# Cross attention's output projection by pairs of k-tiles and 1024 columns, six of its sixteen pieces by seven block products

## The chip, the cores and the metric

One NeuronCore of a Trainium2 chip runs the whole program. The metric is the device time of one launch in microseconds (us). Before the change it is 1568.43 us, the median of three runs (1567.85 to 1570.91).

## What is computed

One layer of an encoder on 256 tokens of width 2048, in float32: a token mixer, cross attention into 256 memory tokens, and a gated convolutional feed-forward network (FFN), each followed by a LayerNorm of `alpha * x + f(x)`. What matters here is the second of the three:

```python
def cross_attention(x, mem, wq, wk, wv, wo):
    ...
    s = jnp.einsum('bqhd,bkhd->bhqk', q, k).astype(jnp.float32) * (XATTN_HEAD_DIM ** -0.5)
    p = jax.nn.softmax(s, axis=-1)
    o = jnp.einsum('bhqk,bkhd->bqhd', p.astype(v.dtype), v).reshape(B, S, D_MODEL)
    return o @ wo

x = layer_norm(DEEPNORM_ALPHA * x + cross_attention(...), ln2_g, ln2_b)
x = layer_norm(DEEPNORM_ALPHA * x + conv_ffn(x, w_up, conv_w, conv_b, w_down), ln3_g, ln3_b)
```

The product `o @ wo` is 256 x 2048 times 2048 x 2048. It is called the output projection, or `xo`, below.

## The kernel before

**Products in three parts.** Every float32 factor of a large product is split into a high part of reduced precision (`hi`, a copy on ACT) and the rest (`lo`, a subtraction on DVE), `split`, lines 84 to 86. A product is then hi x hi + hi x lo + lo x hi, three matmuls of 512 columns each (`three`, line 358; the same three stand in `tok_steps`, lines 286 to 288).

**Slots.** The program is a list of slots (`slot`, line 141; `run`, line 184). A slot has one or more weight loads and a body of matmuls. A load (`Load`, line 96) is one transfer of at most 1 MB by SP's queue into one of three `raw` buffers, then its splits on ACT and DVE into buffers of a pool of 38 (`unit`, line 62). Ahead of each slot, `advance` (line 173) puts the transfers and splits of later loads into the program: `ahead` says how many loads beyond the slot's own are split by then. A background list (`pump`, line 165) puts a piece of attention work ahead of a slot. The framework's scheduler starts from this order and may move an instruction forward where, by its own reckoning, the engine would stand idle; each engine then runs its instructions in the order it was given.

**xo before.** `block_output` (line 924) makes four passes over 512 columns each; a pass has four pieces of 512 rows x 512 columns, one piece to a slot, with 24 matmuls (`tok_steps`, line 280: two blocks of 128 tokens, four k-tiles, three matmuls). `ahead` is 1. The last three pieces of the last pass share a slot, in which token block 0 is finished first (`last_ones`, line 308): its residual sum, its norm (`after_block`, line 1184) and its transposes (`inside`, line 1197, put in front of the last 12 matmuls) go on beside the matmuls of block 1. The heads of attention (`attend`, line 1063) are background work: the last two of four come ahead of the first and third slots of xo. Per pass and token block, `add_residual` (line 896) adds the accumulator to `res` and takes statistics.

**The FFN's down product.** `columns_1024` (line 372) goes by 1024 columns: a piece is two k-tiles x 1024 columns, that is, a 2 x 2 block matrix of weights against a 2 x 2 block matrix of activations (two token blocks by two k-tiles). An *eight* piece has 8 block products, 24 matmuls, one load of 1 MB. A *seven* piece uses Winograd's form of Strassen's method with 7 block products, 21 matmuls. It needs four sums of weight blocks and four sums of activation blocks. The weight sums come from a table in HBM that the program itself makes (`weight_sums`, line 332): six transfers on POOL's queue for each piece, of 0.25 or 0.5 MB, four of them with an add. So a seven piece has two loads, 0.75 MB of weights and 1 MB of sums. In a pass, four accumulators take the seven pieces' first four products; after the last seven piece, `early` (line 1241) adds these into `res` by one ACT and eight DVE operations. Four more accumulators hold the rest of the sums up to the pass's end, where `evac` (line 1262) adds them.

**Pacing of the table.** `make_sums` (line 350) issues one step of the table in each slot from `SUMS_FROM` = 18 on: a DVE copy that reads the slot's first weights, a POOL copy that reads its result, and then the transfer. There are 22 seven pieces, so 132 steps. In slot numbers, xo has slots 117 to 130, the FFN's up product 131 to 172, the first half's down product 173 to 192.

Of the kernel before, what the change touches and what calls it, by code (L numbers as in the profile page):

```python
# [11 lines left out]
F32R = mybir.dt.float32r  # L12
# [8 lines left out]
P = 128  # L21
D = 2048
S = 256
# [18 lines left out]
PAIRS = NF // 2 // HALVES  # L42
SEVEN = ((5, 5), (6, 6))

SUMS_FROM = 18


AFFINE_ON_DVE = ((0, 1, 0), (0, 1, 1), (1, 0, 1))
# [4 lines left out]
def tile_encoder_layer(ctx: ExitStack, tc: tile.TileContext, aps, out):  # L53
# [315 lines left out]
        cols = slice(i * 512, i * 512 + 512)  # L369
        return pair[0][:, cols], pair[1][:, cols]  # L370

    def columns_1024(pieces, sums, act, act_sums, seven, evac_early, evac, stagger):


        rest = [i for i in range(len(pieces)) if i not in seven]
        order, free = [], len(rest) - stagger
        for n, i in enumerate(seven):
            order += [i] + rest[n * free // len(seven):(n + 1) * free // len(seven)]
        order += rest[free:]
        one, two = {}, {}  # L380

        def into(d, key, tag):
            start = key not in d
            if start:
                d[key] = bank("acc", tag)
            return d[key], start

        def seven_body(i):
            def body(ws, ts):
                w11, (w22, w21) = ws[0], (block_of(ws[1], 0), block_of(ws[1], 1))  # L390
                (t1, t3), (t2, t4) = ([block_of(t, j) for j in range(2)] for t in ts)
                x, s = act[i], [(act_sums[i][:, 0, j], act_sums[i][:, 1, j]) for j in range(4)]
                stop = i == seven[-1]
                for key, a, b in ((1, x_of(x, 0, 0), w11), (5, s[0], t1), (6, s[1], t2), (7, s[2], t3)):
                    acc, start = into(one, key, "m")
                    three(acc, a, b, start, stop)
                for key, a, b in ((2, x_of(x, 0, 1), w21), (3, s[3], w22), (4, x_of(x, 1, 1), t4)):
                    acc, start = into(two, key, "g")
                    three(acc, a, b, start, False)
            return body  # L400

        def eight(ws, i, t, h, stop):
            acc, start = into(two, ((2, 3), (4, 8))[t][h], "g")
            for kk in range(2):
                three(acc, x_of(act[i], t, kk), block_of(ws[kk], 1 - h), start and kk == 0, stop and kk == 1)

        def eight_body(i):
            def body(ws):
                for t in range(2):
                    for h in range(2):  # L410
                        eight(ws, i, t, h, False)
            return body

        def last_body(*wss):
            ends = order[-stagger:]
            for t in range(2):
                for h in range(2):
                    for i, ws in zip(ends, wss):
                        eight(ws, i, t, h, i == ends[-1])
                    evac(t, h, two[((2, 3), (4, 8))[t][h]])  # L420

        for i in order[:-stagger]:
            if i in seven:
                slot([Load(pieces[i][:, 512:2048], cols=1536), LaterLoad(sums[i])], seven_body(i),
                     (lambda: evac_early(one)) if i == seven[-1] else None)
            else:
                slot([pieces[i]], eight_body(i))
        slot([pieces[i] for i in order[-stagger:]], last_body)


    ident = cp.tile([P, P], F32, name="ident")
# [575 lines left out]
                yield  # L1007


    memT, x1T, oT, x2T = [], [], [], []  # L1010
    KT, QT, V, PT = {}, {}, {}, {}

    def feature_into(d, h, j):
# [21 lines left out]
    def scores(h):  # L1035
# [24 lines left out]
        split(PT[h][:, 0], PT[h][:, 1], r3(tr, 2))  # L1060
        yield

    def attend(h):
        yield
        for i in range(2):
            o = bank("xo", "m")
            for jj in range(2):
                e = slice((2 * i + jj) * P, (2 * i + jj + 1) * P)
                for m in range(2):
                    for n, (x, y) in enumerate(PARTS):  # L1070
                        nc.tensor.matmul(o[:, jj * S:(jj + 1) * S], lhsT=V[h][x][:, m, e], rhs=PT[h][:, y, m],  # L1071
                                         start=m == 0 and n == 0, stop=m == 1 and n == 2)
            t = unit([P, 2, 2, S], F32R, name="act")
            split(t[:, :, 0], t[:, :, 1], r3(o, 2))
            oT.append(t)
        yield

# [49 lines left out]
        return lambda acc: conv(NF + f, acc, done)  # L1127

    def gate_sums(p):
        x = gated[p]  # L1130
        s = x[:, 2:4].rearrange("p a (b c) -> p (a b) c", b=2)
        x11, x21, x12, x22 = (x[:, k, t * P:t * P + P] for k in range(2) for t in range(2))
        for o, a, b, op in ((0, x21, x22, ALU.subtract), (2, x11, x21, ALU.subtract),
                            (1, s[:, 0], x11, ALU.subtract), (3, x12, s[:, 1], ALU.add)):
            nc.vector.tensor_tensor(s[:, o], a, b, op=op)
        gS[p] = unit([P, 2, 4, P], F32R, name="sums")
        split(gS[p][:, 0], gS[p][:, 1], s)

# [58 lines left out]
    def inside(left):  # L1197

        if left == 1:
            transpose(0, 0, 1, 2, 3)  # L1200
            advance_chunks(0, 0, 1, 0, 1, 2, 2, 3, 3)

    def norm_steps(t, c, i):

        if (t, c, i) == (0, 3, 1):
            standardise(n2, 0, 1)
            transpose(1, 0)
            advance_chunks(1, 0, 0)
            standardise(n2, 1, 1)
        elif (t, c, i) == (1, 0, 0):  # L1210
            standardise(n2, 2, 1)
            transpose(1, 1)
            advance_chunks(1, 1, 1)
            standardise(n2, 3, 1)
        elif (t, i) == (1, 0) and c < 3:
# [12 lines left out]

    def down_piece(key):
        half, g, p = key  # L1230
        return aps["down"][(2 * half + g) * PAIRS + p]

    def down(half):
# [1 line left out]
        if half:  # L1235
            n3["gb"], n3["params"] = [], [None, None]
        for g in range(2):
            def z_of(t, h, g=g):
                return res[:, t, (2 * g + h) * 512:(2 * g + h + 1) * 512]

            def early(b, z=z_of):

                def add(t, h, x, op=ALU.add):
                    y = z(t, h)
                    nc.vector.scalar_tensor_tensor(y, in0=y, scalar=1.0 if half else ALPHA, in1=x,
                                                   op0=ALU.mult, op1=op)

                def add_more(t, h, x, op):
                    nc.vector.tensor_tensor(z(t, h), z(t, h), x, op=op)

                u = unit([P, 2, 512], name="usum")
                nc.scalar.copy(u[:, 0], b[1])
                add(0, 0, b[1])
                add(0, 1, b[5])
                add(1, 1, b[5])
                nc.vector.tensor_tensor(u[:, 0], u[:, 0], b[6], op=ALU.add)
                nc.vector.tensor_tensor(u[:, 1], u[:, 0], b[7], op=ALU.add)
                add_more(0, 1, u[:, 0], ALU.subtract)
                add(1, 0, u[:, 1])
                add_more(1, 1, u[:, 1], ALU.subtract)  # L1260

            def evac(t, h, acc, g=g, z=z_of):
# [8 lines left out]
            columns_1024([down_piece((half, g, p)) for p in range(PAIRS)],  # L1271
                         [lambda key=(half, g, p): made[key] for p in range(PAIRS)],
                         Part(gT, half * PAIRS), Part(gS, half * PAIRS), list(range(SEVEN[half][g])), early, evac,
                         4 if half and g else 2)
            if half and g == 0:
                then(lambda: load_gb(n3, 2))

    for half in range(HALVES):
# [20 lines left out]
    return w.reshape(k // 512, 4, P, c // 512, 512).transpose(3, 0, 2, 1, 4).reshape(-1, P, 2048)  # L1299


def _by_block(w):


    w = w.reshape(HALVES, PAIRS, 2, P, 2, 2, 512).transpose(0, 4, 1, 3, 2, 5, 6)
    return w[:, :, :, :, (0, 0, 1, 1), (1, 0, 1, 0)].reshape(-1, P, 2048)


# [8 lines left out]
def _layout(i):  # L1317
# [19 lines left out]
    a["xo"] = _by_column(i["xo_w"][0])  # L1337
    a["up"] = _by_feature(i["ffn_up"][0])
    a["down"] = _by_block(i["ffn_down"][0])
# [23 lines left out]
```

## Time and profile before

| | |
|---|---|
| median of three runs | 1568.43 us |
| the profiled execution's own time | 1569.4 us |
| its span in the profile | 1567.6 us |
| PE (TensorE matmul) busy | 1547.9 us, 99% |
| PEld (its weight loads) busy | 1334.5 us, 85% |
| DVE (VectorE) busy | 1110.2 us, 71% |
| ACT (ScalarE) busy | 807.4 us, 52% |
| POOL (GpSimd) busy | 170.8 us, 11% |
| DMA | 362.78 MB, mean 231 GB/s |

PE is TensorE's matmuls, whose ends are modelled: a matmul of 512 columns stands in the trace with 389 ns, and the next one starts before that is over. So what a matmul costs in a full stream is read from the distance of the starts.

### The profile page before, as it was taken

What the parts mean: (1) busy time and instruction counts of PE and PEld (TensorE: products, weight loads), DVE (VectorE), ACT (ScalarE), POOL (GpSimd) and SP (SyncE); (2) the same over time, 40 slices, a digit from 0 to 9 for tenths busy, and PEclk for the clock granted to TensorE, in tenths of its full rate; (3) what the DMA queues carried; (4) which work ended last, traced back from release to release, by engine and by line L of the source; (5) the groups of instructions that cost most, each with busy time, mean ns of one, the idle gap of its engine ahead of it and who ended that gap; (6) DMA issues with size and microseconds to landing.
All of it is one profiled execution on the core that took longest, in us unless ns stands there. A gap on an engine that the chain in (4) does not pass through costs nothing.

```text
span 1567.6 us, 21463 instructions
## 1 busy us (share of the span) xinstructions
PE 1547.9 (99%) x8258; PEld 1334.5 (85%) x8258; DVE 1110.2 (71%) x1715; ACT 807.4 (52%) x1187; POOL 170.8 (11%) x288
## 2 busy tenths in 40 slices
PE   9999999999999999999999999999999999999996
PEld 7888888888888888988889888888888888888875
DVE  6568468667765776555657888877778787777768
ACT  5453353456553344444436566666465555556542
POOL 0003113121211111111201220000000000000000
PEclk9999999999999999999999999999999999999998
DMA  8569668887879678767972986555686454545883
GB/s 310 189 239 282 206 230 263 225 256 252 240 193 310 242 232 256 216 192 228 311 253 82 256 271 225 220 194 213 245 321 249 189 192 184 188 177 203 284 322 116
DMA packets 65159, 362.78 MB, mean 231 GB/s; under 512 B 7832, under 2 KB 8224, under 8 KB 30624
## 3 DMA queue, kind: packets, MB, share of 16 engines
q1 hardware_dynamic: 48544, 314.21, 54.5%
q0 software_dynamic: 16512, 47.20, 15.1%
q8 instruction: 65, 1.06, 0.3%
q14 instruction: 38, 0.31, 0.1%
HBM read 359.27 MB, written 48.24 MB: 260 GB/s over the span
## 4 chain that ended last, share of the span: by engine, by line
PE 95%; DVE 2%; DMA 2%; ACT 0%; issue 0%; SPq 0%; DVEq 0%; ACTq 0%
PE acc L224 35%; PE acc L226 18%; PE acc L286 8%; PE acc L287 8%; PE acc L288 8%; PE acc L361 4%; PE acc L362 4%; PE acc L360 4%; DMA raw<-wsum 1%; PE xs L1041 1%; PE xo L1071 1%; PE lev L664 1%; DMA raw<-in_down_dram 0%; PE acc L235 0%; DVE wlo L86 0%; PE acc L242 0%
## 5 line engine op out<-in xcount | busy, mean ns | idle before, releaser
L86 DVE TENSOR_TENSOR wlo<-raw,whi 128x1024 fp32r<-128x1024 f32 (+1 forms) x562 | 666.9, 1213 | 190.4 <-ACT whi L85 166.7
L85 ACT CAST whi<-raw 128x1024 fp32r<-128x1024 f32 (+1 forms) x562 | 566.1, 1043 | 222.6 <-PE acc L287 38.6
L224 PE MATMUL acc<-act,whi 128*128 128x512 f32 x2384 | 573.3, 392 | 2.0 <-DVE act L86 1.8
L224 PEld LDWEIGHTS acc<-act,whi 128*128 128x128 f32 x2384 | 438.8, 189 | 88.6 <-DVE act L86 2.3
L226 PEld LDWEIGHTS acc<-act,wlo 128*128 128x128 f32 x2384 | 306.9, 191 | 12.2
L226 PE MATMUL acc<-act,wlo 128*128 128x256 f32 x2384 | 310.6, 283 | 0.0
L286 PE MATMUL acc<-whi,act 128*128 128x512 f32 x448 | 175.7, 392 | 0.0
L288 PE MATMUL acc<-whi,act 128*128 128x512 f32 x448 | 174.5, 389 | 0.0
L287 PE MATMUL acc<-wlo,act 128*128 128x512 f32 x448 | 174.4, 389 | 0.0
L355 POOL COPY marks<-marks 128x1 f32<-128x1 f32 x132 | 76.1, 580 | 628.8 <-DVE marks L354 628.8
L246 ACT COPY half<-acc 128x256 f32<-128x256 f32 x144 | 52.9, 368 | 114.3 <-PE acc L226 113.4
L288 PEld LDWEIGHTS acc<-whi,act 128*128 128x128 f32 x448 | 84.1, 188 | 17.7
L286 PEld LDWEIGHTS acc<-whi,act 128*128 128x128 f32 x448 | 84.2, 188 | 16.9
L287 PEld LDWEIGHTS acc<-wlo,act 128*128 128x128 f32 x448 | 84.2, 188 | 16.7
L360 PE MATMUL acc<-whi,act 128*128 128x512 f32 x220 | 84.8, 390 | 1.2 <-ACT whi L85 1.2
L362 PE MATMUL acc<-whi,act 128*128 128x512 f32 x220 | 85.6, 389 | 0.0
L361 PE MATMUL acc<-wlo,act 128*128 128x512 f32 x220 | 85.4, 390 | 0.0
L1097 ACT ACTIVATE cy<-hbuf,convp 128x256 f32<-128x256 f32 x88 | 52.9, 601 | 44.2 <-DVE hbuf L247 44.2
L1098 DVE SCALAR_TENSOR_TENSOR cy<-hbuf,convp,cy 128x256 f32<-128x256 f32 x88 | 42.3, 482 | 25.5 <-ACT cy L1097 25.5
L286 PE MATMUL acc<-whi,mixT 128*128 128x512 f32 x128 | 50.0, 390 | 0.0
L360 PEld LDWEIGHTS acc<-whi,act 128*128 128x128 f32 x220 | 41.2, 188 | 10.2 <-ACT whi L85 1.6
L288 PE MATMUL acc<-whi,mixT 128*128 128x512 f32 x128 | 49.8, 389 | 0.0
(246 smaller groups left out, 1363.6 us busy)
## 6 DMA issues: line engine op xcount, KB each, us to landing
raw<-in_up_dram SPq DMA_DIRECT2D x88, 1024.0 KB, 4.8
raw<-in_w_ws_dram SPq DMA_DIRECT2D x29, 1024.0 KB, 6.4
raw<-in_w_xs_dram SPq DMA_DIRECT2D x24, 1024.0 KB, 6.7
wsum<-in_down_dram POOLq DMA_DIRECT2D x44, 512.0 KB, 9.8
raw<-wsum SPq DMA_DIRECT2D x22, 1024.0 KB, 5.4
raw<-in_down_dram SPq DMA_DIRECT2D x22, 1024.0 KB, 5.3
raw<-in_down_dram SPq DMA_DIRECT2D x22, 768.0 KB, 5.7
raw<-in_xk_dram SPq DMA_DIRECT2D x16, 1024.0 KB, 5.9
```

Source lines behind the costliest of these rows:

```text
L85: nc.scalar.copy(hi, src)
L86: engine.tensor_tensor(lo, src, hi.bitcast(F32), op=ALU.subtract)
L224: nc.tensor.matmul(acc, lhsT=hi, rhs=flat(x), start=k == 0, stop=False)
L226: nc.tensor.matmul(acc[:, 0:S], lhsT=lo, rhs=x[:, 0], start=False, stop=k == KD - 1)
L246: nc.scalar.copy(half, acc[:, S:2 * S])
L286: nc.tensor.matmul(acc[t], lhsT=x[:, 0, ts], rhs=hi[:, cols], start=first and j == 0, stop=False)
L287: nc.tensor.matmul(acc[t], lhsT=x[:, 0, ts], rhs=lo[:, cols], start=False, stop=False)
L288: nc.tensor.matmul(acc[t], lhsT=x[:, 1, ts], rhs=hi[:, cols], start=False, stop=last and j == 3)
L355: seen = nc.gpsimd.tensor_copy(marks[:, 8 + i:9 + i], marks[:, i:i + 1])
L360: nc.tensor.matmul(acc, lhsT=x[0], rhs=w[0], start=start, stop=False)
L361: nc.tensor.matmul(acc, lhsT=x[0], rhs=w[1], start=False, stop=False)
L362: nc.tensor.matmul(acc, lhsT=x[1], rhs=w[0], start=False, stop=stop)
```

## The change

The output projection uses `columns_1024`: two passes of 1024 columns, eight pieces each, of which pieces 0, 1 and 2 go by seven block products. The weights in HBM are laid out anew for it on the host (`_by_block`). The two heads of attention that stood between xo's slots are all issued ahead of its first slot (`finish()`). `attend` takes the sums of the activations for the first three pieces (`pair_sums`, the former body of `gate_sums`). `early` becomes `early_into`, with the scale as an argument. In the last slot, with three pieces, the transposes of block 0 stand again in front of the last 12 matmuls. `ahead` is 2 in all slots of `columns_1024`, 3 in xo's last slot. The table of sums has 28 pieces, xo's six first, in 168 steps, and begins in slot 10. Xo has 13 slots instead of 14.

```diff
-SUMS_FROM = 18
+SEVEN_XO = 3
+
+SUMS_FROM = 10
...
+                        if inside and t == 1 and h == 1:
+                            inside(len(ends) - 2 - ends.index(i))
                     evac(t, h, two[((2, 3), (4, 8))[t][h]])
...
-        slot([pieces[i] for i in order[-stagger:]], last_body)
+        slot([pieces[i] for i in order[-stagger:]], last_body, ahead=3 if inside else 2)
...
+    def pair_sums(x):
+
+        s = x[:, 2:4].rearrange("p a (b c) -> p (a b) c", b=2)
+        x11, x21, x12, x22 = (x[:, k, t * P:t * P + P] for k in range(2) for t in range(2))
+        for o, a, b, op in ((0, x21, x22, ALU.subtract), (2, x11, x21, ALU.subtract),
+                            (1, s[:, 0], x11, ALU.subtract), (3, x12, s[:, 1], ALU.add)):
+            nc.vector.tensor_tensor(s[:, o], a, b, op=op)
+        sums = unit([P, 2, 4, P], F32R, name="sums")
+        split(sums[:, 0], sums[:, 1], s)
+        return sums
...
-            split(t[:, :, 0], t[:, :, 1], r3(o, 2))
+            if len(oT) < SEVEN_XO:
+                x = unit([P, 4, S], name="xsum")
+                nc.scalar.copy(x[:, 0:2], r3(o, 2))
+                split(t[:, :, 0], t[:, :, 1], x[:, 0:2])
+                oS.append(pair_sums(x))
+            else:
+                split(t[:, :, 0], t[:, :, 1], r3(o, 2))
...
-    block_output(aps["xo"], 4, oT, n2, 1, after=after_block, inside=inside, affine=False)
+    finish()
+    n2["params"] = [None, None]
+    for g in range(2):
+        def xo_evac(t, h, acc, g=g):
+            y = z_of(g)(t, h)
+            nc.vector.tensor_tensor(y, y, acc, op=ALU.add)
+            nc.vector.bn_stats(stats[t][:, 2 * g + h], y)
+            if g == 1 and h == 1:
+                n2["params"][t] = norm_params(t)
+                after_block(t)
+
+        columns_1024([aps["xo"][8 * g + p] for p in range(8)], [lambda key=("xo", g, p): made[key] for p in range(8)],
+                     oT, oS, list(range(SEVEN_XO)), early_into(z_of(g), ALPHA), xo_evac, 3 if g else 2,
+                     inside if g else None)
...
-    weight_sums([(half, g, p) for half in range(HALVES) for g in range(2) for p in range(SEVEN[half][g])], down_piece)
+    weight_sums([("xo", g, p) for g in range(2) for p in range(SEVEN_XO)]
+                + [(half, g, p) for half in range(HALVES) for g in range(2) for p in range(SEVEN[half][g])], down_piece)
```

The order of the pieces by slots becomes 0, 3, 1, 4, 2, 5, (6, 7) in the first pass and 0, 1, 3, 2, 4, (5, 6, 7) in the second.

## Rows read from the trace of the kernel before

**Rows 1.** The page: the span, the engines' busy time, and TensorE's granted clock by slices.
```profile
span 1567.6 us, 21463 instructions
...
PE 1547.9 (99%) x8258; PEld 1334.5 (85%) x8258; DVE 1110.2 (71%) x1715; ACT 807.4 (52%) x1187; POOL 170.8 (11%) x288
...
PEclk9999999999999999999999999999999999999998
```

**Rows 2.** What PE waited for over the whole span: total us, times, longest.
```profile
PE acc L360 <- ACT whi L85: 2.3, 2, 1.2
...
PE ntr L976 <- DVE res L969: 0.4, 1, 0.4
```

**Rows 3.** Busy time by stretch: us, PE, PEld, DVE, ACT, POOL, PEclk, DMA share, GB/s.
```profile
736.00:830.00 94.00, 94.00 (x447) 79.03 (x446) 60.68 (x88) 39.77 (x48) 15.59 (x28) 1.00 0.78 252
...
1070.00:1180.00 110.00, 110.00 (x502) 91.74 (x501) 80.77 (x91) 62.48 (x72) 0.00 (x0) 1.00 0.73 268
```

**Rows 4.** PE in order of time, late in xo.
```profile
819.77 0.39 PE L286 MATMUL acc<-whi,act 128*128 128x512 f32 x1
...
820.45 0.39 PE L286 MATMUL acc<-whi,act 128*128 128x512 f32 x1
```

**Rows 5.** PE in order of time, first half's down product: where a seven piece begins.
```profile
1094.93 0.39 PE L360 MATMUL acc<-wone,act 128*128 128x512 f32 x1
...
1105.13 0.39 PE L360 MATMUL acc<-wone,act 128*128 128x512 f32 x1
```

**Rows 6.** The page's costliest groups: the subtraction on DVE in a split of 1024 columns.
```profile
L86 DVE TENSOR_TENSOR wlo<-raw,whi 128x1024 fp32r<-128x1024 f32 (+1 forms) x562 | 666.9, 1213 | 190.4 <-ACT whi L85 166.7
```

**Rows 7.** Single lines and tiles: instructions, ns min/median/max, first and last start.
```profile
L86 DVE TENSOR_TENSOR wone<-raw,wone x22: 675/686/693, 1062.7 to 1518.2; 128x512 fp32r<-128x512 f32 x22
L1245 DVE SCALAR_TENSOR_TENSOR res<-res,acc x12: 678/680/687, 1118.2 to 1531.4; 128x512 f32<-128x512 f32 x12
L1135 DVE TENSOR_TENSOR gated<-gated x44: 278/291/294, 873.0 to 1332.5; 128x128 f32<-128x128 f32 x44
```

**Rows 8.** The chain of work that ended last: the last head of attention.
```profile
751.07 2.87 PE xo L1071 x24
```

**Rows 9.** ACT in order of time, around the first slots of xo.
```profile
734.65 0.59 ACT L85 CAST xv<-acc 128x512 fp32r<-128x512 f32 x1 [5.70 <-issue]
735.13 2.00 ACT L85 CAST whi<-raw 128x1024 fp32r<-128x1024 f32 x2
...
754.46 5.79 ACT L85 CAST whi<-raw 128x1024 fp32r<-128x1024 f32 x6
```

**Rows 10.** DVE in order of time, after the last head of attention.
```profile
755.55 4.63 DVE L86 TENSOR_TENSOR wlo<-raw,whi 128x1024 fp32r<-128x1024 f32 x4 [0.26 <-ACT whi L85]
```

**Rows 11.** DMA: a queue's packets, MB and share; issues with KB and us to landing.
```profile
q0 software_dynamic: 16512, 47.20, 15.1%
...
raw<-wsum SPq DMA_DIRECT2D x22, 1024.0 KB, 5.4
...
raw<-in_xo_dram SPq DMA_DIRECT2D x16, 1024.0 KB, 7.3
```

**Rows 12.** The POOL copy in front of each step of the table.
```profile
L355 POOL COPY marks<-marks x132: 183/197/2775, 111.5 to 943.1; 128x1 f32<-128x1 f32 x132
```

**Rows 13.** Busy time by stretch, columns as in rows 3: three shorter stretches.
```profile
760.00:810.00 50.00, 50.00 (x222) 41.41 (x221) 37.07 (x48) 24.37 (x25) 12.63 (x22) 1.00 0.98 343
1500.00:1530.00 30.00, 26.84 (x112) 20.00 (x111) 21.22 (x21) 17.90 (x21) 0.00 (x0) 1.00 0.80 290
1079.90:1105.10 25.20, 25.20 (x113) 20.89 (x112) 17.95 (x20) 15.36 (x19) 0.00 (x0) 1.00 0.71 259
```

**Rows 14.** DVE in order of time, during `early` in the first half's down product.
```profile
1120.01 0.68 DVE L1256 TENSOR_TENSOR usum<-usum,acc 128x512 f32<-128x512 f32 x1
1120.61 1.22 DVE L86 TENSOR_TENSOR wlo<-raw,whi 128x1024 fp32r<-128x1024 f32 x1
```

**Rows 15.** DVE in order of time, xo's last slot.
```profile
822.01 0.69 DVE L898 SCALAR_TENSOR_TENSOR res<-res,acc 128x512 f32<-128x512 f32 x1 [10.19 <-PE acc L288]
```

More of the change, by code (lines that the diff above doesn't have):

```diff
@@ L370, in block_of, with columns_1024 @@
         return pair[0][:, cols], pair[1][:, cols]
-    def columns_1024(pieces, sums, act, act_sums, seven, evac_early, evac, stagger):
+    def columns_1024(pieces, sums, act, act_sums, seven, evac_early, evac, stagger, inside=None):
         rest = [i for i in range(len(pieces)) if i not in seven]
@@ L424, in columns_1024 @@
                 slot([Load(pieces[i][:, 512:2048], cols=1536), LaterLoad(sums[i])], seven_body(i),
-                     (lambda: evac_early(one)) if i == seven[-1] else None)
+                     (lambda: evac_early(one)) if i == seven[-1] else None, ahead=2)
             else:
-                slot([pieces[i]], eight_body(i))
-        slot([pieces[i] for i in order[-stagger:]], last_body)
+                slot([pieces[i]], eight_body(i), ahead=2)
+        slot([pieces[i] for i in order[-stagger:]], last_body, ahead=3 if inside else 2)
     ident = cp.tile([P, P], F32, name="ident")
@@ L1007, in affine @@
                 yield
-    memT, x1T, oT, x2T = [], [], [], []
+    memT, x1T, oT, x2T, oS = [], [], [], [], []
     KT, QT, V, PT = {}, {}, {}, {}
@@ L1129, in gate_sums @@
     def gate_sums(p):
[L1130 to L1137, printed above, removed]
+        gS[p] = pair_sums(gated[p])
     def run_start():
@@ L1201, in inside, with z_of, early_into, early @@
             advance_chunks(0, 0, 1, 0, 1, 2, 2, 3, 3)
+    def z_of(g):
+        return lambda t, h: res[:, t, (2 * g + h) * 512:(2 * g + h + 1) * 512]
+    def early_into(z, scale):
+        def early(b):
+            def add(t, h, x):
+                y = z(t, h)
+                nc.vector.scalar_tensor_tensor(y, in0=y, scalar=scale, in1=x, op0=ALU.mult, op1=ALU.add)
+            def add_more(t, h, x, op):
+                nc.vector.tensor_tensor(z(t, h), z(t, h), x, op=op)
+            u = unit([P, 2, 512], name="usum")
+            nc.scalar.copy(u[:, 0], b[1])
+            add(0, 0, b[1])
+            add(0, 1, b[5])
+            add(1, 1, b[5])
+            nc.vector.tensor_tensor(u[:, 0], u[:, 0], b[6], op=ALU.add)
+            nc.vector.tensor_tensor(u[:, 1], u[:, 0], b[7], op=ALU.add)
+            add_more(0, 1, u[:, 0], ALU.subtract)
+            add(1, 0, u[:, 1])
+            add_more(1, 1, u[:, 1], ALU.subtract)
+        return early
     def norm_steps(t, c, i):
@@ L1230, in down_piece @@
         half, g, p = key
+        if half == "xo":
+            return aps["xo"][8 * g + p]
         return aps["down"][(2 * half + g) * PAIRS + p]
@@ L1237, in down, with evac @@
         for g in range(2):
[L1238 to L1262, printed above, removed]
+            def evac(t, h, acc, g=g, z=z_of(g)):
                 y = z(t, h)
@@ L1272, in down @@
                          [lambda key=(half, g, p): made[key] for p in range(PAIRS)],
-                         Part(gT, half * PAIRS), Part(gS, half * PAIRS), list(range(SEVEN[half][g])), early, evac,
+                         Part(gT, half * PAIRS), Part(gS, half * PAIRS), list(range(SEVEN[half][g])),
+                         early_into(z_of(g), 1.0 if half else ALPHA), evac,
                          4 if half and g else 2)
@@ L1299, in _by_column, with _by_block @@
     return w.reshape(k // 512, 4, P, c // 512, 512).transpose(3, 0, 2, 1, 4).reshape(-1, P, 2048)
-def _by_block(w):
-    w = w.reshape(HALVES, PAIRS, 2, P, 2, 2, 512).transpose(0, 4, 1, 3, 2, 5, 6)
+def _by_block(w, halves):
+    w = w.reshape(halves, -1, 2, P, 2, 2, 512).transpose(0, 4, 1, 3, 2, 5, 6)
     return w[:, :, :, :, (0, 0, 1, 1), (1, 0, 1, 0)].reshape(-1, P, 2048)
@@ L1336, in _layout @@
     a["xv"] = _by_column(i["xv_w"][0])
-    a["xo"] = _by_column(i["xo_w"][0])
+    a["xo"] = _by_block(i["xo_w"][0], 1)
     a["up"] = _by_feature(i["ffn_up"][0])
-    a["down"] = _by_block(i["ffn_down"][0])
+    a["down"] = _by_block(i["ffn_down"][0], HALVES)
     conv = np.concatenate([i["conv_w"][0], i["conv_b"]])
```

## The prediction

> **What bounds the kernel now.** I read the page first: PE is busy for 1547.9 of 1567.6 us at a granted clock of nine tenths or more in all slices but the last [rows 1]. 1.00 of full speed is 2.4 GHz; nothing in the xo stage leaves that level [rows 3]. Then the list of waits: over the whole launch PE's waits on other engines are a few us, and the one that belongs to xo is 0.4 us behind its end, for the first transposes of token block 1 [rows 2]. The table of stretches says the same of the stage: from 736 to 830 us PE is busy for 94.00 of 94.00 us, while DVE has 60.68 and ACT 39.77 [rows 3]. So xo is bound by the number of matmuls, and only fewer of them can shorten it. The same table shows what stands nearest: the DMA engines' share is 0.78 there and 0.98 from 760 to 810 us [rows 3, 13].
>
> **What a matmul costs.** Three matmuls start within 0.68 us, so one is 0.2267 us [rows 4]. From one seven piece to the second next, over 21 + 24 = 45 matmuls, the first half's down product takes 10.20 us, again 0.2267 each [rows 5]: the seven form has no overhead of its own on PE. The Trainium skill (TensorE: Matmul & The Clock Gate, Back-to-back issue gap) gives about 131 ns for 512 columns in a sustained stream, by which 18 matmuls would be an estimated 2.4 us; the trace does not agree, so 227 ns stands.
>
> **The change, part by part.** The sum is made against the profiled execution (span 1567.6 us, 1569.4 us with what lies around it). The median is 1.0 us below that execution, and I apply the difference to it.
>
> *Fewer matmuls.* Each of 16 pieces has 24; six now have 21. 18 x 0.2267 = 4.08 us come off PE's path. This is also the most that the change can give: PE waits for nothing in the stage, so there is no idle time to recover.
>
> *Attention moved.* The last two heads keep PE for 2.87 us each wherever they stand [rows 8]: nothing. But the splits for xo's second load, the sums of piece 0, come behind both heads in program order, since `ahead` is still 1 in the slot before. At worst they start as ACT and DVE did behind the last head before: that head ends at 751.07 + 2.87 = 753.94, ACT's first cast starts at 754.46 and takes about a sixth of 5.79 us, DVE's first subtraction ends about 1.2 us after 755.55 [rows 8 to 10]. The first sum's high part is then there 1.6 us after the head, its low part 2.8 us, the second sum's 4.0 us. PE has three matmuls (0.7 us) that don't need them and waits 0.9, 1.0 and 0.5 us: 2.4 us. At best nothing is lost: before, the second load's cast stood at 735.13, directly behind the first of the two casts of the last values [rows 9], ahead of its place in the program. The row is about the same place in the queue, so I take 0.4.
>
> *More transfers in xo.* Six pieces bring 0.75 MB more each (1 MB here is 1024 KB): 4.7 million bytes. The table's steps go on at one per slot; the software queue carries little else, 15.1% of the span over 132 steps, or 1.79 us of all DMA engines per step [rows 11, 12]. With the table running, a load of xo lands after 7.3 us; without it, a load of sums takes 5.4 [rows 11]: the difference is about one such step. The dense stretch is the first five slots of a pass (three seven, two eight; 25.2 us of PE). The same five pieces in the down product, without the table, took a DMA share of 0.71 and cost PE nothing [rows 13]. Five steps add 5 x 1.79 / 25.2 = 0.36: 1.07, which is 1.7 us too much per stretch. Three raw buffers filled beforehand, over 2 us each at 343 GB/s [rows 13], cover that, and the eight pieces behind it refill them. Below nothing it can't go; the upper end is the one stretch where PE did starve for weights, 3.2 us of 30 in the second half's down product [rows 13]. The nearest rows are the down product's without a stall, so I take 0.5 for both passes.
>
> *More DVE work in xo.* A seven piece's splits are 0.69 + 3 x 1.21 = 4.3 us, an eight piece's 2.4 [rows 6, 7]: six times 1.9 = 11.4. `early` has eight operations of 0.68 a pass [rows 7]: 10.9 in both. That is 83 of some 90 us. The sums of the activations, four of 0.29 and a split for each of three pieces [rows 7], are 5.6 us in the slots of the values, where DVE and ACT waited for PE's accumulators [rows 9]; without that cover they would be at most as long. In the second pass `early` stands one slot ahead of the last, in front of the splits of pieces 6 and 7. If it runs as one block, DVE has 5.5 us and two splits (4.9) to do within the slot of piece 4 (5.4 us) and the first matmuls of the next: up to 5 us late. In the down product the scheduler put splits between the operations of `early` [rows 14], and PE lost nothing there [rows 3]. I take 0.3.
>
> *The end of xo.* Before, DVE had split everything, FFN weights included, and idled 10.2 us until block 0's accumulator was done [rows 15]. 4.7 million bytes at 343 GB/s are 13.8 us of transfer; one slot less saves a step (1.8), and PE comes 4.1 us earlier. So 10.2 - 13.8 + 1.8 - 4.1 = -5.9: the FFN's third load is now split some 6 us after block 0 wants its residual sum. This is what is late next. Where that split stands in front of the norm on DVE, the transposes of block 0 wait, and the up product behind them: up to 5.9. Where the norm goes first, nothing: the first use of the low part is in block 1. The scheduler can choose, and I take 1.0.
>
> *The table itself.* It now runs from slot 10 to 177. Xo's sums are done by slot 58, long before 117. Beside the up product the table ran until 943 us without a wait of PE's [rows 2, 12]; six steps now fall into the first slots of the down product (172 to 177), the dense pattern again with 0.71 of share: 0 to 3.2 us, as above, and I take 0.2, for the two loads split ahead. The first slots without the table (10 to 17) gain steps in a kernel bound by PE: nothing, for the same reason.
>
> Sum: -4.1 + 0.4 + 0.5 + 0.3 + 1.0 + 0.2 = -1.7 us. The profiled execution would take 1567.7, and the median becomes 1566.7.
>
> **The rivals.** About 0.2%, 3.1 us, is what a measurement of this kernel can tell from no change.
>
> *All covers hold.* The scheduler places every split in time and stalls stay under 0.9 us: 1564.3 to 1565.2. For it speaks the down product, the same code with the same density and no lost time [rows 3, 5]. Against it: there the table did not run, and it started from two loads ahead.
>
> *Slower: the DMA engines become the bound in the dense stretches.* Two in xo and one at the start of the down product run with the table's steps between their loads. If each loses what the second half lost, 3.16 us, that is 9.5 - 4.1 = +5.4, or 1573.8 us. It decides against the change as soon as the three lose over 7.2 us together, and is no loss while three raw buffers stay filled. For it speak the share of 1.07 and the 7.3 us to landing; against it that PE lost nothing at 0.98 [rows 13]. The Trainium skill (DMA: Bandwidth & Descriptors, Queues, rings and completion order) says that each DMA engine takes turns between the queues that have work; by it the table would not yield to the loads. The longer landing beside the table agrees.
>
> *The forecast.* Small waits, above all at xo's start and end, take back a part: 1565.3 to 1571.5, most likely 1566.7.
>
> **How the numbers follow.** The forecast has 0.48, the covers 0.32, the slower case 0.20. Within 0.2% (1565.3 to 1571.6) is the forecast, so same 0.48, faster 0.32, slower 0.20. The range leaves out little of the covers below and most of the slower case above: 1564.2 to 1572.0. The likeliest case alone spans 1565.3 to 1571.5.
>
> **What would show it.** Right: 18 matmuls fewer, 227 ns between starts, a new wait of PE at xo's first slot for a high or low part of under 1 us, a DVE without its 10 us gap in xo's last slot, and a wait of PE for the transposes of block 0 or 1 somewhat above 0.4 us. The DMA share should stand near 1 from xo's first to its last slot. Wrong on the one side: no wait of PE in xo and a span 4 us shorter. Wrong on the other: ACT's casts waiting for loads in each dense stretch and PE with 2 or 3 us of idle time in each.

## The result, and the profile after the change

The changed kernel takes 1578.32 us, the median of four runs (1577.04 to 1579.25); the kernel before took 1568.41 in the four runs beside them (1567.85 to 1570.91). The ratio is 1.0055, with a 95% interval of 1.0043 to 1.0067: **slower by some 9 us** (9.9 by these medians, 8.6 by the ratio), above the whole predicted range. The profiled execution took 1577.77 us, of which the span is 1575.9, 8.3 more than before.

The page of the changed kernel, beside [rows 1, 11, 12]:

```profile
span 1575.9 us, 21634 instructions
...
PE 1549.2 (98%) x8240; PEld 1330.1 (84%) x8240; DVE 1137.2 (72%) x1794; ACT 821.8 (52%) x1207; POOL 218.8 (14%) x360
...
q0 software_dynamic: 20928, 59.79, 18.5%
```

PE has 18 matmuls fewer, as the change says, and its busy time rose all the same. The table has 168 steps, and its queue 18.5% of the DMA time, where it had 15.1%.

To see where the time went I cut the span at four starts of PE. The cuts are the end of the values (where the last two heads begin, or in the kernel before the third), the transposes of token block 1 behind xo, the first matmul on `wone` in the first half's down product and in the second half's, and the last matmul; some 13 us behind it stand in no column. The same table serves the experiments below, so their rows stand here too; all are from each kernel's profiled execution, in us.

| kernel | to the values' end | two heads, xo, its end | up product | first down product, second up | second down product | span |
|---|---|---|---|---|---|---|
| before | 737.1 | 100.0 | 242.8 | 357.8 | 116.4 | 1567.6 |
| the change | 738.1 | 109.5 | 242.8 | 357.8 | 114.6 | 1575.9 |
| e2_pause | 737.8 | 100.5 | 242.8 | 369.5 | 118.5 | 1582.2 |
| e4_ahead3 | 740.4 | 101.0 | 243.1 | 357.8 | 116.3 | 1571.7 |
| e5_both | 737.8 | 97.0 | 243.0 | 369.9 | 115.5 | 1576.3 |
| e7_two | 738.2 | 108.1 | 242.8 | 357.8 | 114.5 | 1574.6 |
| e8_two_pauses | 739.0 | 97.0 | 243.0 | 357.8 | 115.5 | 1565.4 |
| e9_two_pauses_18 | 736.2 | 97.0 | 243.0 | 357.8 | 112.8 | 1560.0 |
| e10_move_only | 736.4 | 100.0 | 243.1 | 357.8 | 118.1 | 1568.9 |
| e11_late_up | 736.4 | 96.0 | 246.6 | 357.8 | 115.6 | 1565.5 |
| e12_before_pause | 736.3 | 100.0 | 242.8 | 357.8 | 115.3 | 1565.6 |
| e3_from18 | 737.3 | 112.2 | 242.8 | 358.6 | 117.0 | 1581.0 |

Against before, the change loses 1.0 us ahead of xo and 9.5 in xo's stage, and has 1.8 less in the last column and 0.4 less behind the last matmul: 8.3. The last column moves between 112.8 and 118.5 from kernel to kernel although none of the experiments' edits touches that stage, so its 1.8 can't be put down to the change. The second column is the one to explain: with 4.1 us of matmuls taken away, 9.5 more means 13.6 us of new idle or slow time.

PE's waits over the whole span, beside [rows 2] (total us, times, longest):

```profile
PE acc L363 <- DVE wlo L88: 3.0, 5, 1.5
PE acc L362 <- ACT whi L87: 2.6, 4, 1.5
...
PE ntr L980 <- DVE res L973: 1.5, 1, 1.5
...
PE acc L228 <- DVE wlo L88: 0.9, 1, 0.9
```

Lines 362 to 364 are the three matmuls of `columns_1024`; PE now waits there for split weights. The stretches around xo's start, first of the kernel before and then of the changed one (columns as in [rows 3]):

```profile
732.00:748.00 16.00, 16.00 (x84) 13.72 (x83) 9.86 (x13) 8.03 (x10) 2.16 (x6) 1.00 0.84 207
748.00:770.00 22.00, 22.00 (x110) 18.70 (x109) 15.54 (x20) 10.87 (x12) 4.82 (x8) 1.00 0.96 302
```

```profile
732.00:748.00 16.00, 15.78 (x92) 13.48 (x90) 6.53 (x10) 6.85 (x10) 0.86 (x2) 1.00 0.24 66
748.00:770.00 22.00, 19.56 (x84) 15.24 (x83) 13.28 (x17) 9.86 (x12) 3.69 (x8) 1.00 0.95 274
770.00:783.00 13.00, 13.00 (x51) 10.41 (x50) 10.12 (x13) 7.59 (x9) 0.00 (x0) 0.87 0.81 305
783.00:810.00 27.00, 25.51 (x113) 20.95 (x112) 23.17 (x32) 13.16 (x14) 9.33 (x12) 1.00 0.85 293
810.00:840.00 30.00, 26.99 (x123) 21.25 (x122) 27.34 (x46) 13.47 (x16) 2.68 (x6) 1.00 0.94 333
```

From 748 us on both kernels keep the DMA engines full, at 0.96 and 0.95. But before, PE lost nothing at that share, and now it does. The difference lies just ahead: from 732 to 748 us the DMA share was 0.84 and is now 0.24. Xo begins without a lead. SP's queue shows the hole from the side of the loads:

```profile
721.24 0.33 SPq L109 DMA_DIRECT2D raw<-wsum  x1
723.51 8.87 SPq L109 DMA_DIRECT2D raw<-in_xo_dram  x2
748.04 0.33 SPq L109 DMA_DIRECT2D raw<-wsum  x1
```

The second of the two loads at 723.51 is issued about 732, and then nothing for 16 us. The three `raw` buffers are full, and ACT, which would empty them, is held by something else:

```profile
735.61 0.59 ACT L87 CAST xv<-acc 128x512 fp32r<-128x512 f32 x1 [4.84 <-PE acc L290]
...
739.76 0.59 ACT L87 CAST act<-xo 128x512 fp32r<-128x512 f32 x1 [0.85 <-PE xo L1086]
...
744.57 3.90 ACT L87 CAST whi<-raw 128x1024 fp32r<-128x1024 f32 x4
...
752.90 2.00 ACT L87 CAST whi<-raw 128x1024 fp32r<-128x1024 f32 x2 [2.96 <-DMA raw<-wsum]
...
762.35 0.62 ACT L87 CAST wone<-raw 128x512 fp32r<-128x512 f32 x1 [3.57 <-DMA raw<-in_xo_dram]
```

The casts of the loads that have landed come behind the evacuations of the values and of both heads, and those wait for PE. At 744.57 ACT empties what lies there in one go, and from then on it waits for a transfer before nearly every load. Where PE pays most for it in the first pass (PE in order of time; the idle time of the engine and its releaser stand in brackets):

```profile
767.37 0.49 PE L362 MATMUL acc<-whi,sums 128*128 128x512 f32 x1 [1.50 <-ACT whi L87]
768.63 0.50 PE L363 MATMUL acc<-wlo,sums 128*128 128x512 f32 x1 [0.77 <-DVE wlo L88]
...
771.44 0.63 PE L364 MATMUL acc<-whi,sums 128*128 128x512 f32 x1
771.87 0.63 PE L362 MATMUL acc<-whi,act 128*128 128x512 f32 x1
```

By distances of starts beyond 0.2267 us, xo's matmuls lose 0.6 us at the first slot (746.6), 3.3 in the third seven piece (767 to 770), 1.5 right behind it because the matmuls then start 0.43 us apart, 1.8 at 784.7 and 2.3 at 821 to 824: 9.5 of the 9.8 us by which the stage from 743.88 to 836.68 exceeds its 366 matmuls (83.0). The other 3.9 are behind xo's end. There the order on DVE answers to [rows 15]:

```profile
829.86 0.68 DVE L1266 TENSOR_TENSOR res<-res,acc 128x512 f32<-128x512 f32 x1
...
832.28 2.36 DVE L88 TENSOR_TENSOR wlo<-raw,whi 128x1024 fp32r<-128x1024 f32 x2 [1.01 <-ACT whi L87]
834.55 0.26 DVE L908 BATCH_NORM_AGGREGATE mv<-stats 128x2 f32<-128x24 f32 x1
...
837.71 1.92 DVE L973 TENSOR_SCALAR res<-res,mv,lny 128x512 f32<-128x512 f32 x4
```

The split of a late load of FFN weights, for which DVE idles 1.01 us, stands in front of block 0's norm, and the transposes wait for `res`. The idle 10 us of before are gone. On PE:

```profile
838.31 2.03 PE L980 MATMUL ntr<-ident,res 128*128 128x128 f32 x16 [1.48 <-DVE res L973]
841.31 3.48 PE L237 MATMUL acc<-act,whi 128*128 128x256 f32 x26 [0.98 <-DVE act L88]
```

The text on the change says that block 0's transposes stand in front of xo's last 12 matmuls. That is the program's order; in the trace they run behind all 366. So no matmul of xo covers them, and the up product's first matmuls wait 0.98 us for the split copies of their result.

### The profile page after: what moved, and what is told of

It reads as the page before. It is cut to its first block, busy times and chain, and to the rows that moved or that the text cites. A ratio compares the mean times of both kernels' runs of the same rounds, so it can differ in the third digit from the quotient of the medians.

```text
span 1575.9 us, 21634 instructions
## 1 busy us (share of the span) xinstructions
PE 1549.2 (98%) x8240; PEld 1330.1 (84%) x8240; DVE 1137.2 (72%) x1794; ACT 821.8 (52%) x1207; POOL 218.8 (14%) x360
## 3 DMA queue, kind: packets, MB, share of 16 engines
q0 software_dynamic: 20928, 59.79, 18.5%
## 4 chain that ended last, share of the span: by engine, by line
PE 88%; DMA 6%; DVE 4%; ACT 1%; issue 1%; SPq 0%; DVEq 0%; ACTq 0%
PE acc L226 34%; PE acc L228 18%; PE acc L288 6%; PE acc L289 6%; PE acc L290 6%; PE acc L363 4%; PE acc L364 4%; PE acc L362 4%; DMA raw<-in_xo_dram 2%; DVE wlo L88 2%; DMA normw<-in_norm_w_dram 1%; DMA raw<-wsum 1%; ACT whi L87 1%; PE xo L1086 1%; PE xs L1045 1%
## 5 line engine op out<-in xcount | busy, mean ns | idle before, releaser
L88 DVE TENSOR_TENSOR wlo<-raw,whi 128x1024 fp32r<-128x1024 f32 (+1 forms) x568 | 674.1, 1213 | 187.1 <-ACT whi L87 169.9
L87 ACT CAST whi<-raw 128x1024 fp32r<-128x1024 f32 (+1 forms) x568 | 572.8, 1043 | 239.8 <-PE acc L289 41.8
L357 POOL COPY marks<-marks 128x1 f32<-128x1 f32 x168 | 100.9, 600 | 855.3 <-DVE marks L356 855.3
L288 PE MATMUL acc<-whi,act 128*128 128x512 f32 x320 | 125.8, 393 | 0.0
L363 PE MATMUL acc<-wlo,act 128*128 128x512 f32 x312 | 122.1, 393 | 3.1 <-DVE wlo L88 2.1
L290 PE MATMUL acc<-whi,act 128*128 128x512 f32 x320 | 124.7, 390 | 0.0
L289 PE MATMUL acc<-wlo,act 128*128 128x512 f32 x320 | 124.6, 389 | 0.0
L364 PE MATMUL acc<-whi,act 128*128 128x512 f32 x312 | 121.7, 390 | 0.0
L362 PE MATMUL acc<-whi,act 128*128 128x512 f32 x312 | 120.5, 391 | 0.4 <-ACT whi L87 0.4
L363 PEld LDWEIGHTS acc<-wlo,act 128*128 128x128 f32 x312 | 58.7, 188 | 18.1 <-DVE wlo L88 4.4
L290 PEld LDWEIGHTS acc<-whi,act 128*128 128x128 f32 x320 | 60.1, 188 | 12.7
L288 PEld LDWEIGHTS acc<-whi,act 128*128 128x128 f32 x320 | 60.1, 188 | 11.9
L289 PEld LDWEIGHTS acc<-wlo,act 128*128 128x128 f32 x320 | 60.2, 188 | 11.9
L362 PEld LDWEIGHTS acc<-whi,act 128*128 128x128 f32 x312 | 58.6, 188 | 13.1 <-ACT whi L87 0.8
L364 PEld LDWEIGHTS acc<-whi,act 128*128 128x128 f32 x312 | 58.7, 188 | 11.9
```

The lines of the kernel that those rows point to most:

```text
L87: nc.scalar.copy(hi, src)
L88: engine.tensor_tensor(lo, src, hi.bitcast(F32), op=ALU.subtract)
L288: nc.tensor.matmul(acc[t], lhsT=x[:, 0, ts], rhs=hi[:, cols], start=first and j == 0, stop=False)
L289: nc.tensor.matmul(acc[t], lhsT=x[:, 0, ts], rhs=lo[:, cols], start=False, stop=False)
L290: nc.tensor.matmul(acc[t], lhsT=x[:, 1, ts], rhs=hi[:, cols], start=False, stop=last and j == 3)
L357: seen = nc.gpsimd.tensor_copy(marks[:, 8 + i:9 + i], marks[:, i:i + 1])
```

## The experiments

Two explanations were left for xo. Either the table's steps, beside loads that are 1.75 MB for a seven piece, ask more of the DMA engines than PE's matmuls leave time for; or the hole ahead of xo does it, by taking the lead with which a dense stretch can be paid. Later runs ask which of the two suffices, and whether a version without both is faster than the kernel before.

**e2_pause** is the changed kernel with no step of the table in xo's slots; its 13 steps come later.

```diff
-        if sums_to_make and state["slot"] >= SUMS_FROM:
+        if sums_to_make and state["slot"] >= SUMS_FROM and not 115 <= state["slot"] <= 130:
```

> The table of weight sums makes no step in slots 115 to 130 (its steps come later), so xo's loads have the DMA engines to themselves. Theory A (lead lost: three raw buffers stand full behind the attention's evacuations, DMA idles for some 16 us ahead of xo, and xo starts with nothing in hand): the first pass still starves, at most 5 of the 14 us come back, about 1573 us. Theory B (contention: the table's 13 steps of about 1.8 us of all DMA engines each, in a stage that has none to spare): 10 us or more come back, 1568 us or less, the DMA share in xo falls well below 1, and loads land in under 6 us instead of 8.2.

Measured: 1583.54 us (1578.43 to 1584.3) against 1569.55 for the kernel before, ratio 1.0083 (1.006 to 1.0106). The total missed what was expected, but the stages are plain: xo's stage fell by 9.0 us, to 100.5, with the hole still there (first row below), and the steps that were put off run into the first half's down product, which takes 11.7 us more. Its stretches, and what PE waited for from 1080 to 1210 us:

```profile
732.00:748.00 16.00, 15.78 (x92) 13.47 (x91) 6.85 (x9) 7.21 (x10) 0.00 (x0) 1.00 0.14 49
748.00:837.00 89.00, 87.08 (x403) 71.24 (x401) 78.22 (x110) 49.50 (x67) 4.31 (x9) 1.00 0.75 278
1080.00:1130.00 50.00, 49.02 (x219) 39.83 (x218) 31.42 (x41) 26.05 (x30) 11.12 (x14) 1.00 0.95 297
```

```profile
PE acc L363 <- DVE wlo L88: 5.8, 4, 2.6
```

So the steps are a necessary part of the loss in xo, and they carry a loss with them to the next dense stretch. Contention was expected to give back 10 us or more and landings under 6 us; it is 9.0 us, and xo's loads of 1 MB land after 7.0 us (8.2 in the changed kernel).

One stretch of the changed kernel shows how a step gets in the way. From 757.5 to 761.0 us its DMA engines have a busy share of 0.95 and move only 107 GB/s. The queues' packets, MB and share there (q0 is the table's, q1 that of the loads):

```profile
q0 software_dynamic: 169, 0.32, 88.3%
q1 hardware_dynamic: 20, 0.05, 6.6%
```

The table's two steps in this stretch are adds of 0.25 MB, issued at 752.39 and 753.05. A load of 0.75 MB issued about 752.0 lands 10.3 us later. In e2, without steps, the two loads of that size between 748 and 770 us land after 6.3 us, and ACT casts the first of them at 758.24, where the changed kernel does at 762.35:

```profile
758.24 0.61 ACT L87 CAST wone<-raw 128x512 fp32r<-128x512 f32 x1
```

**e4_ahead3** is the changed kernel in which the last product of the values takes the splits of xo's first sums and of its next piece ahead of its own evacuations, so that two more buffers come free.

```diff
-            product_tok([aps["xv"][4 * h + i] for i in range(4)], memT, value_into(h))
+            product_tok([aps["xv"][4 * h + i] for i in range(4)], memT, value_into(h),
+                        between=lambda i, h=h: set_ahead(3) if (h, i) == (3, 2) else None)
```

> The splits of the sums of piece 0 and of piece 3 go ahead of the last values' and the attention's evacuations; the table runs as before. Theory A: two more loads are under way before xo, about 7 us of transfers, so 6 to 8 us come back, about 1571 us, and the DMA share from 740 to 750 us rises from 0.07 to over 0.5. Theory B: the engines are full anyway from 750 us on; the lead is used up within the first pass and 2 us or less come back, 1576 us or more.

Measured: 1570.97 us (1567.88 to 1573.73), ratio 1.001 (0.9999 to 1.0022). Xo's stage is 101.0, 8.5 less, with the table's steps left where they were; the stage ahead of it is 2.3 longer, of which 0.8 is an early wait that is told of below. The hole is filled:

```profile
732.00:748.00 16.00, 16.00 (x95) 14.22 (x94) 11.29 (x16) 9.41 (x14) 3.00 (x4) 1.00 0.72 214
748.00:840.00 92.00, 88.91 (x408) 74.12 (x407) 76.61 (x116) 48.19 (x65) 14.27 (x29) 0.98 0.82 280
```

PE loses 0.2 us between 740 and 820 us; what remains is the end, where the transposes wait 3.7 us for `res`. So the hole is a necessary part as well.

**e5_both** has both edits.

> Both edits together: no table steps in xo and the two splits ahead. If A and B are both parts of it, all of the loss in xo is gone: PE saves the 4.1 us of 18 matmuls, 1564 to 1566 us. If DVE's order around the early additions were a cause of its own, waits of PE for the low parts remain in the last slots of both passes, 2 us or more, and the time is 1567 or more.

Measured: 1576.81 us (1576.32 to 1578.18), ratio 1.0048 (1.0031 to 1.0066). Xo's stage is 97.0, 12.5 us under the changed kernel's and 3.0 under that of before: 3.0 of the 4.1 us of matmuls arrive. The displaced steps cost 12.1 in the first down product again, so the total misses what was expected.

**e7_two** lets only two pieces of a pass go by seven block products (`SEVEN_XO = 2`): less to load, and 12 matmuls fewer instead of 18.

> Two seven pieces a pass in xo instead of three. PE has six matmuls more, 1.4 us. Where transfers bound xo (A or B), two loads of 0.75 MB less are 4.6 us at 343 GB/s, so the time falls by 3 to 5 us, to about 1574. Where DVE's additions bound it (they are the same in number), it rises by about 1 us, to 1579.

Measured: 1575.01 us (1574.25 to 1576.39), ratio 1.0035 (1.0023 to 1.0046). The total is near the 1574 that was expected if transfers are the bound, but xo's stage, 108.1, is only 1.4 us better, and by another way: PE loses some 1.7 us between 740 and 820 and then waits 6.8 us in one piece for `res`. DVE in order of time at xo's end:

```profile
827.75 2.36 DVE L88 TENSOR_TENSOR wlo<-raw,whi 128x1024 fp32r<-128x1024 f32 x2 [2.19 <-ACT whi L87]
830.03 0.68 DVE L1266 TENSOR_TENSOR res<-res,acc 128x512 f32<-128x512 f32 x1
```

DVE idles 2.19 us for an FFN load and then splits it in front of a residual sum of block 0. So loads that are late show up here even where xo's own matmuls were mostly spared.

**e10_move_only** is the other half of the test: the kernel before, with 16 eight pieces and its old `SUMS_FROM`, in which only the two heads are moved ahead of xo.

```diff
+    finish()
     block_output(aps["xo"], 4, oT, n2, 1, after=after_block, inside=inside, affine=False)
```

> The kernel before with nothing changed but the two heads of attention issued ahead of xo. Theory A says that the hole in the transfers ahead of xo comes from this move, so it must show here too (share under 0.3 between 735 and 748 us); but eight pieces with one load each leave the engines slack, so PE loses 0 to 1.5 us: 1568.5 to 1570.5. If the hole by itself were the cost, it would be 5 us or more, 1574.

Measured: 1570.76 us (1566.51 to 1575.73) against 1569.78, ratio 1.0006 (0.9993 to 1.0019). The hole is there, even emptier, and costs nothing in xo's stage, which is 100.0 as before:

```profile
736.00:748.00 12.00, 12.00 (x77) 10.92 (x76) 7.56 (x9) 8.02 (x11) 0.00 (x0) 1.00 0.13 19
748.00:836.00 88.00, 87.93 (x415) 73.66 (x414) 58.54 (x95) 37.37 (x51) 17.72 (x33) 1.00 0.78 265
```

The queues' shares speak for a reason. From 748 to 840 us, first this kernel (packets, MB, share), then the changed one:

```profile
q1 hardware_dynamic: 2581, 18.79, 52.8%
q0 software_dynamic: 1568, 4.46, 21.5%
```

```profile
q1 hardware_dynamic: 3411, 23.88, 68.4%
q0 software_dynamic: 1616, 3.93, 21.1%
```

With eight pieces the loads (q1) and the table (q0) fill 74.3% of the time; with the six seven pieces 89.5%, as a mean over dense and less dense slots. The Trainium skill (DMA: Bandwidth & Descriptors, Queues, rings and completion order) says that each DMA engine takes turns between queues that have work. The trace agrees in that the table does not yield: its queue has 21.1% of the time while nearly every load is late, and 21.5% where none is. It shows no even turns, though: from 757.5 to 761.0 us the table had 88.3% and the loads 6.6%. And as the slots pace the steps, the mean share alone can't tell turns from another order.

**e8_two_pauses** and **e9_two_pauses_18** put off the table's steps past both dense stretches, xo and the first half's down product, so that they end up beside the second half's up product, and keep the edit of e4. The one starts the table in slot 10, the other in slot 18.

```diff
+SUMS_NOT = ((115, 130), (170, 191))
...
-        if sums_to_make and state["slot"] >= SUMS_FROM:
+        if sums_to_make and state["slot"] >= SUMS_FROM and not any(a <= state["slot"] <= b for a, b in SUMS_NOT):
```

> Both splits ahead, as before, and the table pauses in slots 115 to 130 (xo) and 170 to 191 (first half's down product); its last steps fall into the second half's up product, which has a DMA share of about 0.5. Theory: steps of the table beside seven pieces are what costs, wherever they fall. Then the 12 us that the pause in xo cost in the down product vanish, xo keeps its gain, and the time is 1576.8 - 12 = about 1565 us. Rival: the down product lost its time for another reason (the order that the scheduler chose); then it stays at 1573 or more.

> As the run with two pauses, and the table begins in slot 18 as in the kernel before. Theory: the table's early steps delay a parameter transfer of many small packets beside slots 10 to 17, and with it DVE and PE by about 1 us at 113 us; that wait goes, so 1 us less than the run with two pauses, about 1564. Rival: the start of the program varies by itself, and there is no difference.

Measured: 1564.91 us (1563.25 to 1567.41), ratio 0.9968 (0.9958 to 0.9978), and 1564.65 (1561.74 to 1566.34), ratio 0.9969 (0.9958 to 0.9981). Both are faster than the kernel before and than the changed one. Xo's stage is 97.0 in each, and the first down product costs what it did before. Whether the later start gains the 1 us that was expected of it stays undecided: the two medians differ by 0.3 us, and the ranges overlap. In the second of them:

```profile
732.00:748.00 16.00, 16.00 (x95) 14.22 (x94) 11.05 (x14) 9.40 (x13) 0.00 (x0) 1.00 0.55 199
748.00:840.00 92.00, 91.03 (x451) 76.45 (x450) 77.58 (x117) 49.14 (x76) 5.35 (x9) 1.00 0.68 247
```

**e12_before_pause** asks whether the pauses alone had done that: the kernel before, with no step in its xo slots (`and not 117 <= state["slot"] <= 130` at the same line).

> The kernel before, with no step of the table in its slots 117 to 130 (xo); the 14 steps follow in the up product, where the table then ends some 80 us later, still ahead of the down product. Theory (the steps hurt only where a stretch's transfers with them take longer than PE's matmuls, and with 16 eight pieces they don't): xo's stage stays at 100.0 us, the time within 1.5 us of the kernel before. Rival (what the two versions with pauses gained is owed to the pauses, which would do the same for the kernel before): 2 to 4 us faster than before.

Measured: 1568.45 us (1566.53 to 1572.49) against 1569.28, ratio 0.9996 (0.9987 to 1.0004); xo's stage is 100.0. The pause gives the kernel before nothing. Of the 4.9 and 5.1 us that e8 and e9 gain by their medians, the 3.0 in xo's stage are owed to the 18 matmuls. Where the rest comes from is not shown. One candidate was not tried by itself: `ahead` = 2 in the down products, which the change brings with it (last column 112.8 to 118.5 with it, 115.3 to 118.1 without).

**e11_late_up** tries for the rest of the end: e9 with `ahead` 1 instead of 3 in xo's last slot, so that two of the three FFN loads are split behind the norm.

```diff
-        slot([pieces[i] for i in order[-stagger:]], last_body, ahead=3 if inside else 2)
+        slot([pieces[i] for i in order[-stagger:]], last_body, ahead=1 if inside else 2)
```

> As the run with two pauses from slot 18, but in xo's last slot only one of the three loads of the up product is split ahead, so that no split that waits for a transfer stands in front of block 0's norm on DVE. Theory C (that order is what makes PE wait for the transposes at the end of xo): the wait for res goes, 1 to 3 us less than its twin. Rival: the up product starts without its weights, and PE waits as long or longer for the casts; same or slower by up to 5 us.

Measured: 1566.45 us (1565.63 to 1569.52), ratio 0.9985 (0.9976 to 0.9995): faster than before, but not than e9. The wait for `res` is gone. The cut behind xo falls earlier in the work here, with 24 of the up product's matmuls in front of it instead of 38, so the second and third columns have to be taken together: 342.6 us against 340.0 in e9. PE's waits from 815 to 850 us are for the split copies of the activations, not for the weights that the rival named:

```profile
PE acc L238 <- DVE act L89: 2.0, 1, 2.0
PE acc L238 <- POOL act L89: 1.5, 4, 0.8
```

**e3_from18** is the changed kernel with `SUMS_FROM` back at 18.

> The changed kernel with the table's first step at slot 18 again: eight more steps fall into the first half's down product, beside its dense stretch. Theory (a step beside a dense stretch costs PE about 0.9 us, as 13 displaced steps cost 11.7): the early wait at 113 us is gone (-1), xo's stage stays near 109 us, the down product loses 5 to 8 us: 1582 to 1586 us. Rival (the three raw buffers cover the down product's start, as the six steps that it has now cost nothing): 1577 us.

Measured: 1582.37 us (1581.44 to 1585.68) against 1569.28, ratio 1.0084 (1.007 to 1.0098). The total is as the theory had it, the place is not. The early wait is gone (0.8 less in the first column), but the eight steps that it moves into the first down product cost 0.8 there, not 5 to 8. Xo's stage lost 2.7 more, and the last column 2.4. So a step does not cost a fixed 0.9 us. What differs from e2 in the down product is number and kind. From 1080 to 1130 us the table moved 2.88 MB in e2 and 1.84 MB here (first e2, then e3):

```profile
q0 software_dynamic: 831, 2.88, 29.3%
```

```profile
q0 software_dynamic: 816, 1.84, 18.1%
```

The last 16 steps of a group of four pieces are of 0.25 MB, and the adds ahead of them of 0.5 MB; e2 has four of the latter between 1076 and 1100 us, e3 none. In xo it is the other way: three adds of 0.5 MB fall between 738 and 835 us here, and none in the changed kernel. That size decides is argued from this, not tried by itself. (Three of a piece's six transfers add, not four, as is said further up: lines 342, 344 and 346 of the changed kernel.)

## Why the prediction was wrong

**The step that failed is "More transfers in xo".** It took 0.5 us for both passes, with a claim that three filled `raw` buffers, each worth over 2 us of transfer, cover 1.7 us too much per stretch. The demand was about right. The three seven and two eight pieces are 7.6 MB; at e2's price from 748 to 770 us (7.13 MB in 86.9% of 22 us) they take 20.4 us, and the table's queue had 31.1% of the same 22 us in the changed kernel, 6.8 us. Together that is 27.2 us beside 25.2 of matmuls, 1.08 by this estimate, where 1.07 was forecast. The cover was not there. I took the lead of the kernel before [rows 13] to belong to the stretch, and it belongs to what stands ahead of it: with both heads in front of xo the buffers were full, but of loads whose splits stood behind evacuations that wait for PE, and the transfers stood still for 16 us. Then the loads start from nothing, and xo's matmuls lose 9.8 us, 0.6 of them at the first slot, instead of 0.5. E4 restores the lead and gets 8.5 us back in xo's stage; e2 takes the steps away and gets 9.0; both together give 12.5. E10 has the hole and the steps without the seven pieces and loses none. So it takes the hole and the steps, beside the added loads.

**Attention moved** was costed at 0.4 us for the wait at the first slot, and that measured 0.4 at 746.62 (0.6 with its tail). The step looked for what the move does to the first slot's splits, and not for what it does to the loads behind them: it asked when the splits would be done, where it should also have asked when the buffers come free.

**Fewer matmuls** was right: 18 fewer, 0.2267 us apart. E5, e8 and e9 show 3.0 us of the 4.1 as a shorter stage. The other 1.1 goes at xo's end: there block 0's transposes have only xo's last 5 matmuls behind them, where before they had 12, and the wait for those of block 1 is 0.8 us instead of 0.4. How the 1.1 divides was not tried.

**More DVE work in xo** was taken at 0.3 us. In the changed kernel the stalls at 784.7 and 821 come where `early` stands in front of a split, 4.1 us together. In e5 and e8 the same operations are there and PE loses nothing between 740 and 820 us; so DVE's work is covered when the loads are in time, and these stalls are read as the late loads seen one engine on.

**The end of xo** was taken at 1.0 of up to 5.9 us, with FFN loads split in front of block 0's norm as what is late next. That is what happened, at 3.9 us, within its bounds but nearly four times the term. Of it 1.48 us is the wait for `res` and 0.98 the wait behind the uncovered transposes, which the term didn't have. The 6.8 us of wait in e7 is above the bounds. In e8 and e9, with the loads in time, what is left is 0.8 for block 1 and 0.2 for a split copy.

**The table** was taken at 0.2 us in the down product, where its six steps cost nothing. In the first slots, where it was put at nothing, there is a wait of 0.9 us for a low part at 113.20 and the first column is 1.0 longer. In e4 and e8, which also start at slot 10, that wait is 1.7, in e2, e5 and e7 there is none; no run that starts at slot 18 has it. The first column is 737.8 to 740.4 in the six kernels that start at slot 10 and 736.2 to 737.3 in the six that start at 18, so the early steps seem to cost a little there; as e7 shows (738.2, without that wait), it is not this wait alone, and with one profiled execution each it stays open.

**The rivals.** The slower case named the right mechanism, the DMA engines as the bound in the dense stretches, and gave 1573.8 us for it; what told against it, no loss at 0.98, was a row from a stage that had a lead. It put a third of the loss into the down product's start, which lost nothing, and too little into xo. Its sign for it, casts that wait for loads and PE idle 2 to 3 us in a dense stretch, is in the trace as said for the first one. The share "near 1 from the first to the last slot" is not: it falls to 0.81 and 0.85 in the middle, while ACT still waits for loads. Three buffers, of which each must land, be cast and be split before the next issue, seem not to keep the engines full once the loads are late. That is argued; a fourth buffer was not tried.

## What to carry to other kernels

Before a change adds loads to a stretch, set the DMA time of everything that runs there, background transfers included, against PE's time. Where it is over 1, find the lead that pays for it, and look at the stretch ahead for anything in the splitting engines' order that keeps the buffers full. Background work that is put off must land in a stretch with room, or the loss moves with it.

## What the runs showed of the hardware

Two things I had not expected. Behind 3.3 us of PE's stalls at 767 to 770 us the granted clock of the stretch 770 to 783 is 0.87, and seven matmuls start 0.43 us apart, about twice 0.2267, which is the lower of the two levels (1.2 GHz): 1.5 us that no wait shows. And the second half's down product, which none of the experiments' edits touches, takes from 112.8 to 118.5 us from one kernel's profiled execution to another's; what sets that stayed open, and it is why the stages above say more than the spans.
